# Cached keys turned by VectorE's block transpose, and raw buffers of 1,056 columns, in a hybrid streaming encoder step

## The chip, the core and the metric

The kernel runs on one core of a Trainium2 chip. A core has five engines that run side by side, each in the order of its own instruction list: TensorE (PE in the profile, with its weight loads as PEld), VectorE (DVE), ScalarE (ACT), GpSimd (POOL) and SyncE (SP). SyncE issues every transfer of this kernel; the transfers run on 16 DMA engines, in the order in which they were issued. The metric is the device time of one execution in microseconds; smaller is better.

## The reference

One inference step of a one-layer encoder, width 1024, on a prompt of 1024 rows and on eight running streams with 16 new rows each. All values are float32.

```python
# mixers, on the same normalised input
sq, sk, sv, fq, fk, fv, fg, z, xbc, dt = split_last(u @ w_in, IN_SIZES)
sb_o  = stick_breaking(sq, concat(cache_sb_k, sk), concat(cache_sb_v, sv))   # 4 heads of 64
fox_o = forgetting_softmax(fq, concat(cache_fox_k, fk), ..., log_gates)       # 4 heads of 64
ssd_o = rmsnorm(ssd_scan(...) * silu(z))                                       # 8 heads of 64
h = h + concat(sb_o, fox_o, ssd_o) @ w_out
# cross-attention, 4 heads of 256, 256 memory rows
q = rmsnorm(h) @ wq_x
h = h + softmax(q @ mem_k.T / 16) @ mem_v @ wo_x
# feed-forward
h = h + (silu(u @ w_gate) * (u @ w_up)) @ w_down
```

The prompt has no past. Each of the eight streams has 1024 cached rows of keys and values for both attention mixers, and its own 256 rows of memory keys and values for the cross-attention (`cache_mem_k`, `cache_mem_v`). All caches are stored with rows along the first axis, while a product of queries with keys needs the keys with the head's columns along the 128 partitions. The turning of these cached keys is what the change is about.

## The kernel before

The rows of the prompt and the streams, 1152 together, form nine blocks of 128 (the ninth holds the streams) or three chunks of 384. Dense products run in split precision: each float32 operand becomes a high part in a reduced format and a low part that holds the rest, and a product takes three matmuls (`mm3`, lines 328 to 330: high by high, high by low, low by high). A weight is loaded to a raw buffer, cast by ScalarE to the high part (L292) and subtracted by GpSimd for the low part (L132, in pieces of 256 columns). `w_unit` does this for one unit of weights.

The ring of buffers that all this goes through has four raw buffers of 528 columns (tag `wr`) and three each of 1,056 columns for the high and low parts (`wh`, `wl`). The decode also puts its turned keys (`kf`) and cached values (`vr`) into `wh` and `wl`.

The program is in one Python order with generators woven into each other, and a planner orders each engine's list by priorities and a simulated time line. Four stages touch the change:

- The first decode (stick-breaking, module 0) and the second (FoX, module 1), with prompt attention units around them. Each decode has four units of two streams; each unit calls `load_k` four times, for two halves of the cache and two streams, 32 calls in all. A call loads 512 rows of 256 columns with two transfers (L882), turns them with eight transposes on TensorE into PSUM (L888), and copies them out with two ScalarE copies (L890). Four products of 32 by 512 then run in four column groups of TensorE at once (L873).
- Dense projections fill the first decode; the SSD scan fills the second. It reloads its inputs by transfers from scratch in HBM (`act<-acsc`, `act<-xbcsc`, `act<-zsc`).
- The cross-attention goes head by head. `x_query` projects the queries of one head as two halves of 128 columns, with one weight unit of eight k-tiles by 128 columns for each half, while the attention of the head before is woven in (`both`, from `x_prompt` and `x_sample`).
- `x_sample` treats the eight streams of one head in two passes of four streams. In each pass it loads memory keys of two streams at a time (`mem_rows`, L1558), turns them by eight TensorE transposes (L1578), copies them by ScalarE and VectorE into `kf` (L1580), and multiplies (L1564). After the softmax it does the same with the memory values, which need no turning.

Elsewhere the raw buffers serve the weights of `w_out`, `wq_x` and `wo_x`, and one squares pass writes into one as scratch (L1804).

Of the kernel before, what the change touches and what calls it, by code (L numbers as in the profile page):

```python
# [62 lines left out]
def tile_hybrid_step(ctx: ExitStack, tc: tile.TileContext, a: dict):  # L63
# [239 lines left out]
    def raw_t():  # L303

        return ring.tile([P, 528], F32, tag="wr", name="wr", bufs=4)

    def w_unit(srcs, k0, nk, raw=None, pair=None, eng=POOL):

        n = sum(s[2] for s in srcs)
        raws = [raw_t(), raw_t()] if raw is None else [raw]  # L310
# [10 lines left out]
        for i, r in enumerate(raws):  # L321
            sl = slice(i * nk_ * n, (i + 1) * nk_ * n)
            split_into(hi[:, sl], lo[:, sl], r[:, :nk_ * n], eng)
# [516 lines left out]
    def decode_units(m):  # L840
# [15 lines left out]
        def rows(p):  # L856
# [19 lines left out]
            def load_k(hf, b2):  # L876
                rvs = []
                for q in range(2):
                    rvs.append(raw_t()[:, :512].rearrange("p (k c) -> p k c", c=256))
                    k0 = hf * 512 + q * 256  # L880

                    SP.dma_start(out=rvs[q], in_=ck[2 * p + b2, k0:k0 + 256, :].rearrange("(p k) c -> p k c", k=2))  # L882
                kf = ring.tile([P, 1056], F32, tag=("wh", "wl")[b2], name="kf")
                for q in range(2):
                    tp = pT()
                    for nb in range(2):
                        for k in range(2):
                            PE.transpose(tp[:, (2 * nb + k) * P:(2 * nb + k + 1) * P], rvs[q][:, k, nb * P:(nb + 1) * P],  # L888
                                         ident)
                    ACT.copy(kf[:, :1024].rearrange("c (n q p k) -> c n q p k", n=2, q=2, k=2)[:, :, q],  # L890
                             tp.rearrange("c (n k p) -> c n p k", n=2, k=2))
# [546 lines left out]
    def x_query(hd, out):  # L1438
# [5 lines left out]
        def job(db):  # L1444
# [7 lines left out]
            return ((2 * hd + db) * P, consume)  # L1452
        for db in range(2):
            yield from dense_T(wq, uc, [job(db)])

    def x_softmax(ps, n, pr):
# [3 lines left out]
        for i in range(n):  # L1460
            ACT.activation(pr[:, i * 256:(i + 1) * 256], ps[:, i, :], AF.Exp, bias=mx[:, n + i:n + i + 1],
# [7 lines left out]
    def x_mem(hd):  # L1469
# [78 lines left out]
    def x_sample(hd, q):  # L1548
        qs = q[2]
        for db in range(2):  # L1550
            POOL.tensor_copy(*put_streams(db, qs[:, db, :]))

        def mem_rows(src, b0):
# [3 lines left out]
            for b in range(2):  # L1557
                SP.dma_start(out=rv[:, b], in_=src[(b0 + 2 * b) * 256:(b0 + 2 * b + 1) * 256, hd * 256:(hd + 1) * 256]  # L1558
# [517 lines left out]
```

## Time and profile before

| what | value |
|---|---|
| median of three runs | 1884.5 us (1882.29 to 1886.88) |
| profiled execution | 1882.33 us |
| its span | 1880.6 us |
| granted TensorE clock | 0.994 |
| TensorE busy | 1826.0 us, 97% |
| VectorE, ScalarE, GpSimd busy | 886.7, 802.5, 618.4 us |
| DMA | 296.64 MB in 291,036 packets, 49.9% of 16 engines |

Busy times of different engines overlap, so they don't add up to the span. A row of a group names the line, the engine, the operation, the buffer written and read, the shape, the count, then the busy time in us and the mean of one in ns, then the idle time just before and what ended it. Matmuls are pipelined: the mean of one holds its latency, and the distance from one start to the next is what it costs in a dense row of them. A DMA packet is one contiguous run of bytes.

### The profile page before, as it was taken

How to read it: one execution, taken by the hardware profiler on the slowest of the kernel's cores; microseconds unless marked ns; L12 is line 12 of the kernel's file. 1: busy time of each engine (PE TensorE's matmuls, PEld its weight loads, DVE VectorE, ACT ScalarE, POOL GpSimd, SP SyncE). 2: the span in 40 equal slices, each digit the busy share in tenths (PEclk: the TensorE clock that was granted, in tenths of full speed). 3: DMA queues.
4: the chain of work that ended last, by engine and by line, in shares of the span. 5: the costliest groups of instructions: out<-in, count | busy, mean ns of one | idle time of the engine just before them, and what ended most of it. 6: DMA issues, size and time to landing. Idle time of an engine off the chain costs nothing.

```text
span 1880.6 us, 32355 instructions
## 1 busy us (share of the span) xinstructions
PE 1826.0 (97%) x12136; PEld 1632.1 (87%) x12136; DVE 886.7 (47%) x1798; ACT 802.5 (43%) x1719; POOL 618.4 (33%) x921
## 2 busy tenths in 40 slices
PE   7999998999999999999999989999999999999998
PEld 5899877888967768899988889999999999888886
DVE  3412323475657862444443596333333334455554
ACT  6533543545456861344432464333333333344443
POOL 7622424445116663101112107445444542000000
PEclk9999999999999999999999999999999999999999
DMA  9465654437588882245585124333222223657572
GB/s 333 153 188 152 210 144 130 144 109 205 175 262 266 281 288 91 108 134 177 173 284 191 68 73 119 90 85 76 71 71 71 71 71 93 217 184 246 171 247 86
DMA packets 291036, 296.64 MB, mean 158 GB/s; under 512 B 80060, under 2 KB 242852, under 8 KB 290880
## 3 DMA queue, kind: packets, MB, share of 16 engines
q1 hardware_dynamic: 290880, 294.57, 49.9%
q8 instruction: 96, 1.57, 0.3%
q14 instruction: 60, 0.49, 0.1%
HBM read 225.12 MB, written 69.91 MB: 157 GB/s over the span
## 4 chain that ended last, share of the span: by engine, by line
PE 83%; DMA 5%; DVE 4%; POOL 3%; ACT 2%; issue 2%; SPq 0%; DVEq 0%; POOLq 0%; ACTq 0%
PE psd L1869 11%; PE psd L328 10%; PE psd L329 10%; PE psd L330 10%; PE pst L1869 8%; PE pss L1869 4%; PE pss L328 4%; PE pss L329 4%; PE pss L330 4%; PE pso L1869 2%; PE pst L328 2%; PE pst L329 2%; PE pst L330 2%; PE pso L593 1%; DMA act<-acsc 1%
## 5 line engine op out<-in xcount | busy, mean ns | idle before, releaser
L132 POOL TENSOR_TENSOR wl<-wr,wh 128x256 fp32r<-128x256 f32 (+2 forms) x184 | 142.3, 807 | 229.5 <-ACT wh L292 208.6
L328 PE MATMUL psd<-act,wh 128*128 128x384 f32 x528 | 182.3, 346 | 0.0
L330 PE MATMUL psd<-act,wl 128*128 128x384 f32 x528 | 181.2, 343 | 0.6 <-POOL wl L132 0.6
L329 PE MATMUL psd<-act,wh 128*128 128x384 f32 x528 | 181.7, 344 | 0.0
L1869 PE MATMUL pst<-bT,tr 128*128 128x256 f32 (+1 forms) x1068 | 155.0, 293 | 0.0
L1869 PEld LDWEIGHTS pst<-bT,tr 128*128 128x128 f32 x1068 | 144.9, 188 | 0.1
L330 PE MATMUL psd<-wh,act 128*128 128x512 f32 (+3 forms) x424 | 136.7, 323 | 0.0
L329 PE MATMUL psd<-wl,act 128*128 128x256 f32 (+3 forms) x414 | 134.0, 324 | 1.9 <-POOL wl L132 1.9
L328 PE MATMUL psd<-wh,act 128*128 128x256 f32 (+3 forms) x414 | 132.9, 325 | 0.7 <-DMA act<-osc 0.5
L1869 PE MATMUL psd<-bT,tr 128*128 128x320 f32 (+1 forms) x912 | 132.8, 295 | 0.6 <-POOL tr L132 0.6
L1869 PEld LDWEIGHTS psd<-bT,tr 128*128 128x128 f32 x912 | 124.7, 188 | 1.0 <-POOL tr L132 0.9
L132 POOL TENSOR_TENSOR tr<-u,tr 128x256 fp32r<-128x256 f32 x110 | 82.8, 781 | 101.7 <-ACT tr L1705 83.8
L253 POOL TENSOR_SCALAR sm<-sm 128x1 f32<-128x1 f32 (+2 forms) x27 | 9.1, 337 | 298.4 <-ACT y L1980 209.0
L1844 DVE TENSOR_TENSOR tr<-tr,pst 128x256 f32<-128x256 f32 (+1 forms) x86 | 38.6, 449 | 139.9 <-ACT tr L1841 106.6
L330 PEld LDWEIGHTS psd<-act,wl 128*128 128x128 f32 x528 | 99.2, 188 | 3.2 <-issue 1.9
L132 POOL TENSOR_TENSOR ws<-ws 128x256 f32<-128x256 f32 (+2 forms) x100 | 69.2, 719 | 98.7 <-DVE ws L522 90.4
L328 PEld LDWEIGHTS psd<-act,wh 128*128 128x128 f32 x528 | 99.4, 188 | 2.5 <-issue 1.8
L329 PEld LDWEIGHTS psd<-act,wh 128*128 128x128 f32 x528 | 99.3, 188 | 1.9 <-issue 1.5
L132 POOL TENSOR_TENSOR tr<-raw,tr 128x256 fp32r<-128x256 f32 x94 | 69.2, 764 | 83.8 <-ACT tr L1705 75.7
L1705 ACT CAST tr<-u 128x512 fp32r<-128x512 f32 x130 | 76.8, 620 | 28.6 <-PE pst L1869 5.6
L292 ACT CAST wh<-wr 128x512 fp32r<-128x512 f32 (+2 forms) x90 | 52.4, 621 | 82.9 <-PE psd L330 32.1
L329 PEld LDWEIGHTS psd<-wl,act 128*128 128x128 f32 x414 | 78.9, 191 | 10.0 <-POOL wl L132 3.6
(645 smaller groups left out, 4674.4 us busy)
## 6 DMA issues: line engine op xcount, KB each, us to landing
u<-w_down SPq DMA_DIRECT2D x40, 512.0 KB
raw<-w_down SPq DMA_DIRECT2D x26, 512.0 KB
st<-qksc SPq DMA_DIRECT2D x48, 256.0 KB
wr<-w_in SPq DMA_DIRECT2D x44, 256.0 KB
tr<-hidsc SPq DMA_DIRECT2D x55, 192.0 KB
hidsc<-tr SPq DMA_DIRECT2D x34, 288.0 KB
qksc<-sg SPq DMA_DIRECT2D x48, 192.0 KB
wr<-cache_sb_k SPq DMA_DIRECT2D x32, 256.0 KB
```

Of the source, the lines that this page charges most:

```text
L132: POOL.tensor_tensor(out=out[:, a0:a1], in0=in0[:, a0:a1], in1=in1[:, a0:a1], op=op)
L253: POOL.tensor_scalar(v, ss, inv, EPS, ALU.mult, ALU.add)
L292: ACT.copy(hi, raw)
L328: PE.matmul(out, ah, bh, start=start, stop=False)
L329: PE.matmul(out, ah, bl, start=False, stop=False)
L330: PE.matmul(out, al, bh, start=False, stop=stop)
L593: return PE.matmul(po[r:r + 64, q_], vt[:, 2 * (k0 + i) + j, :], pfs[i][:, sl], start=start and k0 == 0 and (j == 0 or qp > 0), stop=k0 + ...
L1705: ACT.copy(hi, src)
L1844: DVE.tensor_tensor(out=at(out, g), in0=at(x, g), in1=ps[g][:, :GW[g]], op=op)
L1869: PE.matmul(dst[g][:, :GW[g]], x[:, ka], y[:, k, :], start=start and k == 0 and m == 0, stop=stop and k == 3 and m == 2, skip_group_check= ...
```

## The change

Three things change together.

The 32 calls of `load_k` load the same 512 rows with four transfers instead of two, one for each group of 32 partitions, so that partition and column already hold the right 32 by 32 blocks; each run in HBM is 32 floats long. One VectorE block transpose (`DVE.transpose`, which turns every 32 by 32 block of a 128 by 1024 tile by itself) writes the turned keys. The TensorE transposes and ScalarE copies go.

`x_sample` does the same for the memory keys, with four transfers in runs of 64 floats per two streams and one block transpose in its own buffer, and its products read every second column of it. The order of columns that follows (even columns of the head in the first half, odd ones in the second) is met by the query weights: `x_query` now loads both halves of a head as two units of four k-tiles by 256 columns, and `split_parted` sorts even and odd columns while it splits. The streams' order within a head and the memory rows' order in the softmax are permuted to match, in instructions that were there before. `kf` no longer takes `wh` and `wl` in `x_sample`.

The raw buffers become two of 1,056 columns, and `w_unit` uses the halves of one.

```diff
     def raw_t():
-        return ring.tile([P, 528], F32, tag="wr", name="wr", bufs=4)
+        return ring.tile([P, 1056], F32, tag="wr", name="wr", bufs=2)
+    def split_parted(hi, lo, raw):
+        h, l = (t.rearrange("p (k x m) -> p k x m", x=2, m=P) for t in (hi, lo))
+        r = raw.rearrange("p (k m x) -> p k x m", x=2, m=P)
+        ACT.copy(h, r)
+        for k in range(h.shape[1]):
+            POOL.tensor_tensor(out=l[:, k], in0=r[:, k], in1=f32(h[:, k]), op=ALU.subtract)
...
-        raws = [raw_t(), raw_t()] if raw is None else [raw]
+        if raw is None:
+            raw = raw_t()
+            raws = [raw[:, :528], raw[:, 528:]]
+        else:
+            raws = [raw]
...
             def load_k(hf, b2):
-                rvs = []
-                for q in range(2):
-                    rvs.append(raw_t()[:, :512].rearrange("p (k c) -> p k c", c=256))
-                    k0 = hf * 512 + q * 256
-                    SP.dma_start(out=rvs[q], in_=ck[2 * p + b2, k0:k0 + 256, :].rearrange("(p k) c -> p k c", k=2))
+                raw = raw_t()[:, :1024]
+                src = ck[2 * p + b2, hf * 512:(hf + 1) * 512, :].rearrange("(i t) (n g j) -> g i (t n) j", t=16, n=2, g=4)
+                for g in range(4):
+                    SP.dma_start(out=raw[32 * g:32 * g + 32].rearrange("i (b j) -> i b j", j=32), in_=src[g])
                 kf = ring.tile([P, 1056], F32, tag=("wh", "wl")[b2], name="kf")
-                for q in range(2):
-                    tp = pT()
-                    for nb in range(2):
-                        for k in range(2):
-                            PE.transpose(tp[:, (2 * nb + k) * P:(2 * nb + k + 1) * P], rvs[q][:, k, nb * P:(nb + 1) * P],
-                                         ident)
-                    ACT.copy(kf[:, :1024].rearrange("c (n q p k) -> c n q p k", n=2, q=2, k=2)[:, :, q],
-                             tp.rearrange("c (n k p) -> c n p k", n=2, k=2))
+                DVE.transpose(kf[:, :1024].rearrange("c (n i t) -> c t n i", n=2, t=16), raw)
                 return kf
...
+        units = [w_unit([(wq, 256 * hd, 256)], k0, 4, parted=True) for k0 in (0, 4)]
         for db in range(2):
-            yield from dense_T(wq, uc, [job(db)])
+            _, consume = job(db)
+            for c in range(NCH):
+                ps = pd()
+                uh, ul = uc[c]
+                for k in range(KT):
+                    wh, wl = (t[:, k % 4, db * P:(db + 1) * P] for t in units[k // 4])
+                    mm3(ps[:, :CW], wh, wl, uh[:, k, :], ul[:, k, :], k == 0, k == KT - 1)
+                consume(c, ps[:, :CW])
+                flush()
+                yield
...
             for i0 in (0, 2):
-                rv = mem_rows(cmk, 2 * i0 + e)
-                kf = ring.tile([P, 1056], F32, tag=("wh", "wl")[i0 // 2], name="kf")
-                for b in range(2):
-                    tp = pT()
-                    for db in range(2):
-                        for mb in range(2):
-                            PE.transpose(tp[:, db * 256 + mb * P:db * 256 + (mb + 1) * P],
-                                         rv[:, b, mb, db * P:(db + 1) * P], ident)
-                    (DVE.tensor_copy if b else ACT.copy)(kf[:, b * 512:(b + 1) * 512], tp)
-                kfs.append(kf)
+                raw = ws_t()[:, :1024]
+                k0 = (4 * e + i0) * 256
+                for g in range(4):
+                    SP.dma_start(out=raw[32 * g:32 * g + 32].rearrange("i (t c) -> i t c", c=64),
+                                 in_=cmk[k0:k0 + 512, hd * 256 + 64 * g:hd * 256 + 64 * g + 64]
+                                 .rearrange("(i t) c -> i t c", t=16))
+                blocks = raw.rearrange("p (t j x) -> p t x j", x=2, j=32)
+                DVE.transpose(blocks, blocks)
+                kfs.append(raw.rearrange("p (t i x) -> p x t i", x=2, i=32))
                 if i0:
-                    products(ps, e, lambda i, x: kfs[i // 2][:, i % 2 * 512 + x * 256:i % 2 * 512 + (x + 1) * 256])
+                    products(ps, e, lambda i, x: kfs[i // 2][:, x, :, i % 2 * 16:i % 2 * 16 + 16])
...
-                PE.transpose(tp[:, db * 256 + mb * P:db * 256 + (mb + 1) * P], mkn[:, mb, db * P:(db + 1) * P], ident)
+                PE.transpose(tp[:, db * 256 + mb * P:db * 256 + (mb + 1) * P], mkn[:, mb, db::2], ident)
```

More of the change, by code (lines that the diff above doesn't have):

```diff
@@ L303, in raw_t, with w_unit @@
     def raw_t():
[L305 to L310 removed]
+        return ring.tile([P, 1056], F32, tag="wr", name="wr", bufs=2)
[5 more added lines that the diff above has]
+            POOL.tensor_tensor(out=l[:, k], in0=r[:, k], in1=f32(h[:, k]), op=ALU.subtract)
+    def w_unit(srcs, k0, nk, raw=None, pair=None, eng=POOL, parted=False):
+        n = sum(s[2] for s in srcs)
+        if raw is None:
[3 more added lines that the diff above has]
+            raws = [raw]
         nk_ = nk // len(raws)
@@ L322, in w_unit @@
             sl = slice(i * nk_ * n, (i + 1) * nk_ * n)
-            split_into(hi[:, sl], lo[:, sl], r[:, :nk_ * n], eng)
+            if parted:
+                split_parted(hi[:, sl], lo[:, sl], r[:, :nk_ * n])
+            else:
+                split_into(hi[:, sl], lo[:, sl], r[:, :nk_ * n], eng)
         return (hi[:, :nk * n].rearrange("p (k n) -> p k n", n=n),
@@ L1460, in x_softmax @@
         for i in range(n):
-            ACT.activation(pr[:, i * 256:(i + 1) * 256], ps[:, i, :], AF.Exp, bias=mx[:, n + i:n + i + 1],
+            to, of = pr[:, i * 256:(i + 1) * 256], ps[:, i, :]
+            if blocks:
+                to, of = to.rearrange("q (i t) -> q t i", t=blocks), of.rearrange("q (t i) -> q t i", t=blocks)
+            ACT.activation(to, of, AF.Exp, bias=mx[:, n + i:n + i + 1],
                            accum_out=su[:, i:i + 1])
@@ L1550, in x_sample @@
         for db in range(2):
-            POOL.tensor_copy(*put_streams(db, qs[:, db, :]))
+            dst, _ = put_streams(db, qs[:, db, :])
+            POOL.tensor_copy(dst, qs[:, db, :].rearrange("p (e i t) -> p i e t", e=2, t=DEC_S))
         def mem_rows(src, b0):
@@ L1557, in mem_rows @@
             for b in range(2):
-                SP.dma_start(out=rv[:, b], in_=src[(b0 + 2 * b) * 256:(b0 + 2 * b + 1) * 256, hd * 256:(hd + 1) * 256]
+                SP.dma_start(out=rv[:, b], in_=src[(b0 + b) * 256:(b0 + b + 1) * 256, hd * 256:(hd + 1) * 256]
                              .rearrange("(m p) c -> p m c", p=P))
@@ L1562, in products, with out @@
         def products(ps, e, moving):
-            together([lambda i=i, x=x, b=2 * i + e: PE.matmul(
-                ps[32 * i:32 * i + 32, :256], zq[:, x, 32 * b:32 * b + 32], moving(i, x),
+            def out(i, m):
+                o = ps[32 * i:32 * i + 32, :256]
+                return o if len(m.shape) == 2 else o.rearrange("p (t i) -> p t i", i=DEC_S)
+            together([lambda i=i, x=x, b=2 * i + e, m=moving(i, x): PE.matmul(
+                out(i, m), zq[:, x, 32 * b:32 * b + 32], m,
                 start=e == 0 and x == 1, stop=e == 1 and x == 0) for x in (1, 0) for i in (3, 0, 1, 2)])
@@ L1601, in x_sample @@
         for db in range(2):
-            PE.transpose(tp[:, db * P:(db + 1) * P], on[:, db * P:(db + 1) * P], ident)
+            PE.transpose(tp[:, db * P:(db + 1) * P].rearrange("p (e i t) -> p i e t", e=2, t=DEC_S),
+                         on[:, db * P:(db + 1) * P], ident)
         x_out(hd, (tp[:, 0:P], tp[:, P:2 * P]), SEQ, P)
```

8 lines of the change are left out of this document (4 added, 4 removed).

## The prediction

> **What bounds the kernel now.** I read the page first, its busy shares and its chain of waits, and then the windows of the stages.
>
> ```profile
> span 1880.6 us, 32355 instructions
> ...
> PE 1826.0 (97%) x12136; PEld 1632.1 (87%) x12136; DVE 886.7 (47%) x1798; ACT 802.5 (43%) x1719; POOL 618.4 (33%) x921
> ...
> PE 83%; DMA 5%; DVE 4%; POOL 3%; ACT 2%; issue 2%; SPq 0%; DVEq 0%; POOLq 0%; ACTq 0%
> ```
>
> TensorE is busy 97% of the span and carries 83% of the chain that ended last. Work taken from it is worth its full price where nothing else is close behind. Where that holds is read from the stages: 188 to 435 us holds the stick-breaking decode, 515 to 705 the forgetting (FoX) decode beside the SSD scan, 800 to 990 most of the cross-attention. Each row has the stretch, its length, the busy time (and instructions) of PE, PEld, DVE, ACT and POOL, the granted clock, the DMA share and GB/s.
>
> ```profile
> 188.00:435.00 247.00, 233.21 (x1778) 202.58 (x1776) 110.22 (x191) 116.19 (x269) 100.01 (x156) 0.99 0.51 149
> 435.00:515.00 80.00, 79.37 (x591) 73.80 (x587) 49.06 (x102) 37.72 (x87) 33.49 (x53) 1.00 0.65 190
> 515.00:705.00 190.00, 177.33 (x1471) 134.84 (x1471) 132.83 (x381) 123.69 (x275) 97.67 (x156) 0.99 0.84 275
> 705.00:800.00 95.00, 95.00 (x437) 77.67 (x436) 36.55 (x64) 28.07 (x51) 26.04 (x39) 1.00 0.30 103
> 800.00:990.00 190.00, 189.48 (x1403) 176.57 (x1402) 89.17 (x210) 75.14 (x203) 22.15 (x37) 1.00 0.58 193
> ```
>
> The cross-attention is TensorE's alone: 189.5 of 190 us busy, DMA at 58%. The first decode is nearly so (94%, DMA 51%). The FoX stage is different: TensorE has 12.7 us idle, its weight loads cover only 135 of 190 us, VectorE is at 70%, and the 16 DMA engines are at 84%. Its chain of waits says the same:
>
> ```profile
> by line: DMA act<-acsc 13.4%; issue 5.2%; PE pst L578 4.7%; PE pso L593 4.1%; DMA wr<-cache_fox_k 4.0%; DMA s_ssm<-act 3.0%; DVE act L1079 3.0%; DMA act<-mixsc 2.9%; POOL act L1030 2.8%; DVE act L1085 2.7%; DMA act<-zsc 2.6%; ACT act L1077
> ...
> 514.49 7.56 DMA wr<-cache_fox_k
> ```
>
> There the transfers named add up to 26% of the chain, and one key load takes 7.56 us from issue to use. So this stage must be asked about DMA, the other two about TensorE.
>
> **What is removed.** 256 transposes in `load_k` (L888; 32 calls, 8 each) and 128 in `x_sample` (L1578; 16 units, 8 each), with the copies out of PSUM behind them.
>
> ```profile
> L888 PE MATMUL pst<-ident,wr 128*128 128x128 f32 x256 | 38.2, 278 | 3.9 <-DMA wr<-cache_sb_k 2.7 <-ACT kf L890 0.8 <-DMA wr<-cache_fox_k 0.3
> L890 ACT COPY kf<-pst 128x512 f32<-128x512 f32 x64 | 36.2, 593 | 17.4 <-PE pst L888 13.6 <-PE pss L873 3.2
> L1578 PE MATMUL pst<-ident,ws 128*128 128x128 f32 x128 | 20.7, 273 | 0.0
> L1580 DVE COPY kf<-pst 128x512 f32<-128x512 f32 x16 | 10.9, 687 | 2.5 <-PE pst L1578 1.7 <-PE psd L329 0.5
> L1580 ACT COPY kf<-pst 128x512 f32<-128x512 f32 x16 | 9.4, 589 | 6.9 <-PE pst L1578 6.0 <-PE psd L329 0.7
> L271 DVE TENSOR_SCALAR ws<-ws,sm 128x1024 f32<-128x1024 f32 x9 | 9.0, 1049 | 0.1
> L522 DVE TENSOR_TENSOR_SCAN ws<-ws 128x1024 f32<-128x1024 f32 x4 | 9.5, 2376 | 4.5 <-ACT ws L519 4.5
> L1564 PE MATMUL pss<-kf,ws 128*32 128x256 f32 x128 | 8.6, 385 | 0.0
> ```
>
> Busy time would make it 38.2 + 20.7 = 58.9 us. That is too much, since the busy time of a transpose includes its latency, which the next matmul overlaps. The timeline has the step between starts:
>
> ```profile
> 868.55 0.33 PE L328 MATMUL psd<-act,wh 128*128 128x384 f32 x1
> 868.72 0.34 PE L329 MATMUL psd<-act,wh 128*128 128x384 f32 x1
> 868.90 0.27 PE L1578 MATMUL pst<-ident,ws 128*128 128x128 f32 x1
> 868.92 0.42 PE L330 MATMUL psd<-act,wl 128*128 128x384 f32 x1
> 869.18 0.27 PE L1578 MATMUL pst<-ident,ws 128*128 128x128 f32 x1
> ...
> 341.95 1.03 PE L888 MATMUL pst<-ident,wr 128*128 128x128 f32 x8
> ```
>
> Two dense matmuls stand 0.17 us apart; transpose to transpose with one dense matmul between is 0.28, so a transpose costs 0.11. Eight in a row take 1.03, of which the last one's 0.27 is latency: 0.76/7 = 0.11. I take 0.11 us: 128 transposes are 14 us in each of the three stages, 42 us in all; 58.9 us is the upper end.
>
> ScalarE loses 36.2 + 9.4 us and VectorE 10.9 us of copies, which lie beside TensorE and count for nothing directly.
>
> **What is added on VectorE.** 48 block transposes of 128x1024, 32 for the decodes and 16 for the memory keys. No row shows one. The nearest of that size are a plain pass at 1.05 us (L271) and the scan at 2.38 us (L522); I take 1.1, since a transpose has no dependence from element to element as a scan has. In the FoX stage VectorE goes from 132.8 to 132.8 + 16 x 1.1 = 150 us of 190 (171 at 2.38); in the others it stays under 60%. It is hidden, and in its place the 0.59 us copy and the transposes before it fall away from each chain. Without that cover the price would be 16 x 1.1 = 18 us in the FoX stage. [...]
>
> **What is added on the DMA queue.** A key load was 2 transfers with runs of 2 KB; it becomes 4 with runs of 32 floats, 128 bytes. A memory-key unit goes from 2 transfers with 1 KB runs to 4 with 256-byte runs. The price per packet comes from windows that hold one kind of transfer: 384.3 to 384.8 us (a store of 128-byte runs, L959), 368.0 to 369.6 (a load of 256-byte runs, L510), 421.4 to 423.5 (a key load), 860.4 to 871.8 (memory rows). In each row: packets, MB, share of 16 engines.
>
> ```profile
> q1 hardware_dynamic: 274, 0.03, 43.5%
> ...
> q1 hardware_dynamic: 1040, 0.26, 72.2%
> ...
> q1 hardware_dynamic: 288, 0.52, 80.4%
> ...
> q1 hardware_dynamic: 3264, 3.15, 85.8%
> ```
>
> Share x window x 16 / packets gives 0.435 x 0.5 x 16 / 274 = 12.7 ns for 128 bytes, and likewise 17.8 ns for 256 bytes, 93.8 for 2 KB and 47.9 for 1 KB. These counts include 16 small packets per transfer. A key load was 2 x 144 packets x 93.8 / 16 = 1.7 us of the whole queue and becomes 4 x 1040 x 12.7 / 16 = 3.3 us. For 16 calls of one decode: 27 us become 53, +26. That a load of 128 bytes costs what the store does isn't shown; the 256-byte load bounds it at 17.8 ns without other traffic (74 us, +47), and half of that, 8.9, from below (+10). Memory keys: 16 x 544 x 47.9 / 16 = 26 us become 16 x 2112 x 17.8 / 16 = 38, +12.
>
> First decode: 126 us of DMA become 152 in 247; cross-attention: 110 become 122 in 190. Both are hidden. FoX stage: 0.84 x 190 = 160 become 186 in 190. TensorE alone would now allow 176, DMA needs 186 without a gap: I take the stage as unchanged, 0, between -14 and, at 17.8 ns, 207 - 190 = +17. Every call also issues two more transfers, 96 in all, on the one queue that carries everything. The VectorE transposes stand in order on their engine, so one that waits for its load holds up the SSD and softmax work behind it, where before it was TensorE that waited, little:
>
> ```profile
> L882 SPq DMA_DIRECT2D wr<-cache_fox_k x32: 328/383/2783, 468.5 to 653.4; - x32
> PE pst L888 <- DMA wr<-cache_sb_k: 2.7, 2, 1.5
> ```
>
> At 0.38 us (the median) the 96 issues are 37 us, spread over three stages of 627 us; what they delay is in the DMA sum.
>
> **What is moved.** Query weights come as two units of four k-tiles by 256 columns per head, both held until the second half of the head is done. Of three buffers one is free, so the next head's second unit is split only after the first unit's last use.
>
> ```profile
> L132 POOL TENSOR_TENSOR wl<-wr,wh 128x256 fp32r<-128x256 f32 x176 | 136.2, 806 | 229.5 <-ACT wh L292 208.6 <-PE pst L578 16.0 <-DMA wr<-wq_x 4.8
> L292 ACT CAST wh<-wr 128x512 fp32r<-128x512 f32 x82 | 47.6, 621 | 79.5 <-PE psd L330 32.1 <-DMA wr<-w_in 9.4 <-PE pss L1564 7.9
> ```
>
> The split takes one cast and four subtracts before all is ready, 0.62 + 4 x 0.81 = 3.9 us. Between release and need lie 24 dense matmuls (k 4 to 7 of the last group, k 0 to 3 of the next), 24 x 0.17 = 4.1 us, and attention work: hidden, 1 us at most. Without the cover it is 3 x 3.9 = 12 us. The raw buffers, two of 1,056 for four of 528, come free with the second half's split instead of the first's, two subtracts or 1.6 us later; prefetched loads hide that. The softmax and output permutations keep their instruction counts.
>
> **The sum.** First decode -14, and -1 for waits of TensorE on L888's loads and copies; FoX 0; cross-attention -14 + 1 = -13. Together -28. The profiled execution took 1882.3 us (1.7 around its span): 1854. The median of the runs, 1884.5, is 2 higher, so 1855 is what I expect of a median.
>
> **Rivals.** *B, the FoX stage gives its share too:* loads go out early (the first are issued at 468.5, with DMA at 65% there), and the copies and PSUM tiles no longer waited for shorten its chain: 14 more, 1841, down to about 1830 if the transposes are worth their busy time. Against it: 186 us of transfers in 190. *C, the wait moves to VectorE:* if each of the 16 FoX loads shows its extra 3.3 - 1.7 = 1.6 us on the path, the stage grows by 26: about 1881. For it: the 7.56 us load and the 26% of the chain in transfers; against: `load_k` has two raw buffers and runs ahead.
>
> *D, slower: 128-byte loads are dear.* The FoX stage without its key loads holds 160 - 27 = 133 us of DMA; its new loads are 66,560 packets, 4160 per engine. The gain of 28 is gone once 133 us + 4160 c = 218 us, c = 20.5 ns. At twice the store's price, 25.4 ns, the stage takes 239: +49 - 28 = +21, 1904 us by the profiled execution. For it: these rows are stores or loads in quiet windows, and in the stage the queue is contended. Against: the 256-byte load at 17.8 moves twice the bytes. [...]
>
> **Chances.** Forecast 0.5 (own range 1842 to 1868), B 0.2, C 0.15, D 0.15. The range 1832 to 1884 reaches over B and C and leaves out D and B's far end. A difference under 0.2%, 3.8 us, can't be told from none. Faster: forecast, B and a third of C, 0.75; same: half of C, 0.08; slower: D and the rest, 0.17.
>
> **What would show it.** Right: TensorE's busy time about 50 us lower, the cross-attention and first decode each 13 to 15 us shorter, 128-byte packets near 13 ns, the FoX stage at 98% DMA and as long as before. Wrong: transposes of 2 us or more on VectorE with TensorE idle before L873; L535 or the SSD lines waiting behind them; a FoX stage well over 200 us with DMA above 95% throughout; or TensorE idle before the query matmuls for POOL's splits.

## The result

The change makes the kernel slower: 1928.1 us median of four runs (1923.6 to 1933.7), against 1884.5 before (four runs, 1882.3 to 1886.9). The ratio is 1.023, with a 95% interval of 1.022 to 1.025. The prediction said 1855 us, with a range from 1832 to 1884. The profiled execution took 1923.6 us for 1882.3.

The page of the kernel after:

```profile
span 1921.8 us, 31580 instructions
...
PE 1818.4 (95%) x11752; PEld 1612.9 (84%) x11752; DVE 964.3 (50%) x1830; ACT 762.6 (40%) x1639; POOL 618.6 (32%) x921
...
DMA packets 435929, 296.59 MB, mean 154 GB/s; under 512 B 245436, under 2 KB 395940, under 8 KB 435776
...
q1 hardware_dynamic: 435776, 294.58, 53.9%
```

All 384 transposes are gone from TensorE's count (12,136 to 11,752), but its busy time fell by 7.6 us only, and the span grew by 41.2. So TensorE now waits 49 us more in all, and what work is left takes longer.

I cut the span at three points that can be found in every kernel: the last scan of the first decode (L522 before), the first sum of the output projection (L1322), which ends the FoX stage, and the first feed-forward product (L1869). The feed-forward part behind them takes 786.1 us before and 786.9 after. The columns are the stretch, its length, busy time (and instructions) of PE, PEld, DVE, ACT and POOL, the granted clock, the DMA share and GB/s. First the windows of before, then those of after:

```profile
188.00:455.60 267.60, 253.18 (x1890) 221.15 (x1889) 122.80 (x204) 125.97 (x291) 113.56 (x172) 0.99 0.53 155
455.60:701.60 246.00, 234.07 (x1933) 187.94 (x1932) 165.91 (x462) 149.57 (x334) 117.61 (x192) 0.99 0.78 251
701.60:1094.50 392.90, 391.63 (x2372) 342.19 (x2373) 183.47 (x386) 144.94 (x354) 67.95 (x103) 1.00 0.45 151
```

```profile
188.00:455.60 267.60, 246.72 (x1772) 214.99 (x1765) 152.82 (x219) 111.16 (x262) 118.00 (x175) 0.94 0.60 152
455.60:729.30 273.70, 237.81 (x1803) 184.65 (x1801) 200.77 (x477) 134.76 (x303) 116.15 (x192) 0.92 0.85 225
729.30:1134.90 405.60, 387.69 (x2245) 335.13 (x2245) 189.93 (x388) 136.22 (x338) 67.83 (x104) 0.97 0.50 147
```

Three things can be read from each row: the length, TensorE's idle time (length less busy) and its clock. The record of the granted clock knows two values, 1.0 and 0.5; the column is their mean, so half of the busy time spent at half clock is taken as lost work: in the trace of after, a 128x128 transpose starts 0.11 us behind the one before it at full clock, and 0.21 us at half clock. The first row of the table counts idle time from TensorE's first matmul on.

| stage | length | idle of TensorE | time at half clock |
|---|---|---|---|
| start to end of first decode | 455.6 to 455.6 | 20.2 to 27.5 | 6.8 to 30.7 |
| FoX | 246.0 to 273.7 | 11.9 to 35.9 | 3.4 to 44.4 |
| rest of output projection, cross-attention | 392.9 to 405.6 | 1.3 to 17.9 | 0 to 20.5 |

Take 14 us for the transposes out of each row, add the new idle time and half of the new time at half clock: FoX gives -14 + 24.0 + 20.5 = +30.5 against 27.7 measured, the cross-attention -14 + 16.6 + 10.3 = +12.9 against 12.7, the first decode -14 + 7.3 + 12.0 = +5 against 0. The books close to about 5 us, since part of the half-clock time is idle time and is counted twice here.

Without that part, TensorE is busy at half clock for 22.0, 41.0 and 15.8 us after, and for 6.4, 3.4 and 0 before. With half of this taken off, its busy time falls by 15.5, 14.9 and 11.9 us, 42 in all. This estimate of the work that went is what the prediction had priced. Beside it stand two losses that the prediction had put at nothing: waits of TensorE, and a clock that falls behind them.

### The profile page after: what moved, and what is told of

The parts are those of the page before. It is cut to its first block, busy times and chain, and to the rows that moved or that the text cites. A ratio compares the mean times of both kernels' runs of the same rounds, so it can differ in the third digit from the quotient of the medians.

```text
span 1921.8 us, 31580 instructions
## 1 busy us (share of the span) xinstructions
PE 1818.4 (95%) x11752; PEld 1612.9 (84%) x11752; DVE 964.3 (50%) x1830; ACT 762.6 (40%) x1639; POOL 618.6 (32%) x921
## 5 line engine op out<-in xcount | busy, mean ns | idle before, releaser
L132 POOL TENSOR_TENSOR wl<-wr,wh 128x256 fp32r<-128x256 f32 (+2 forms) x152 | 118.0, 809 | 260.3 <-ACT wh L292 251.0
L342 PE MATMUL psd<-act,wh 128*128 128x384 f32 x528 | 182.7, 346 | 1.0 <-DVE sg L470 1.0
L342 PE MATMUL psd<-wh,act 128*128 128x256 f32 (+3 forms) x414 | 136.7, 334 | 4.8 <-DMA act<-osc 2.8
L342 PEld LDWEIGHTS psd<-act,wh 128*128 128x128 f32 x528 | 99.7, 189 | 5.5 <-issue 1.9
L342 PEld LDWEIGHTS psd<-wh,act 128*128 128x128 f32 x414 | 81.8, 198 | 15.7 <-DMA act<-osc 3.7
L344 PEld LDWEIGHTS psd<-wh,act 128*128 128x128 f32 x424 | 83.4, 197 | 11.2 <-DMA act<-osc 4.1
```

The costliest lines, as they stand in the source:

```text
L132: POOL.tensor_tensor(out=out[:, a0:a1], in0=in0[:, a0:a1], in1=in1[:, a0:a1], op=op)
L342: PE.matmul(out, ah, bh, start=start, stop=False)
L344: PE.matmul(out, al, bh, start=False, stop=stop)
```

## What the new waits look like

These are the groups of after for the new transposes and for the memory products (the 256 of the last row are those with the keys and those with the values):

```profile
L896 DVE STREAM_TRANSPOSE kf<-wr 128x1024 f32<-128x1024 f32 x32 | 61.0, 1940 | 41.8 <-PE psd L343 10.5 <-DMA wr<-cache_sb_k 9.1 <-DMA wr<-cache_fox_k 8.6
...
L1602 DVE STREAM_TRANSPOSE ws<-ws 128x1024 f32<-128x1024 f32 x16 | 19.9, 1244 | 20.6 <-DMA ws<-cache_mem_k 20.4 <-DVE st L1454 0.2
...
L1587 PE MATMUL pss<-ws 128*32 128x256 f32 x256 | 16.4, 387 | 3.1 <-DMA act<-osc 3.1
```

A decode transpose takes 1.94 us and VectorE stands 41.8 us idle ahead of the 32 of them, some of it for loads. What stands behind such a wait is seen in the first decode. VectorE's timeline and a wait of TensorE in the same stretch of after:

```profile
239.43 1.90 DVE L896 STREAM_TRANSPOSE kf<-wr 128x1024 f32<-128x1024 f32 x1 [4.35 <-DMA wr<-cache_sb_k]
241.18 0.17 DVE L506 TENSOR_TENSOR lf<-psd,hb 128x4 f32<-128x4 f32 x2
```

```profile
PE psd L342 <- DVE lf L506: 1.9, 1, 1.9
```

VectorE waits 4.35 us for a key load. Behind it in VectorE's order stands a pass of 0.17 us that empties a PSUM tile (L506), and TensorE's next dense product (L342) waits 1.9 us for that tile. Before, this unit's transposes stood later in time (from 247.7 us on); two of them waited for their load, 1.5 and 1.1 us, and the pass (L492 there) had no transpose ahead of it. In after it is TensorE's only wait between 238.9 and 242.2 us; yet the record of the clock shows half clock for 3.4 us from 242.2 us on.

The largest such place follows. Windows of after, 14, 2, 24 and 12 us long, and then one form of transpose from groups within 276.5 to 299 us and within 312 to 388 us:

```profile
260.00:274.00 14.00, 13.68 (x106) 10.88 (x104) 4.53 (x8) 7.67 (x20) 5.63 (x7) 1.00 0.48 149
274.00:276.00 2.00, 0.00 (x0) 0.00 (x0) 2.00 (x3) 0.93 (x2) 2.00 (x2) 1.00 1.09 366
276.00:300.00 24.00, 15.33 (x65) 12.57 (x66) 18.26 (x42) 6.57 (x15) 15.04 (x28) 0.51 0.46 59
300.00:312.00 12.00, 10.23 (x135) 9.41 (x133) 0.51 (x3) 0.60 (x3) 0.00 (x0) 0.99 0.28 100
```

```profile
L929 PE MATMUL pst<-ident,ws 128*128 128x128 f32 x9 | 2.4, 427 | 3.2 <-POOL ws L132 3.2
...
L592 PE MATMUL pst<-ident,ws 128*128 128x128 f32 x54 | 9.0, 274 | 0.1
```

A stop of 3.2 us is followed by 24 us at half clock, and the same transpose takes 427 ns there and 274 at full clock. Over the 16 traces of this case, of the idle times of TensorE of 2.5 us and more that began at full clock (without the one behind its first matmul), 56 of 61 were followed by half clock within 7 us of their start; of those between 1 and 1.5 us, 36 of 104. In the traces of before and after alone it is 8 of 8 and 2 of 11, and there the stretches at half clock last 3.41, 6.83, 13.65 and 23.89 us, multiples of 3.41, but for one at the very end of each kernel (6.1 and 5.8 us). What makes the clock fall isn't shown, but the stop ahead can be shorter than such a stretch: in the 3.4 us ahead of the fall at 242.2 us, TensorE stood idle for 1.9 us only.

In the FoX stage the products of queries with keys, of the prompt (L574) and of the caches (L887), wait for VectorE's softmax passes (L549), the first of them 12 times (waits of TensorE, and of VectorE's transposes, 456 to 730 us):

```profile
PE pss L574 <- DVE sm L549: 13.7, 12, 2.5
...
PE pss L887 <- DVE sm L549: 3.4, 3, 2.3
```

```profile
DVE kf L896 <- DMA wr<-cache_fox_k: 8.6, 3, 4.2
```

Before, the longest wait of TensorE in that stage was 2.9 us, and of the two lines' matmuls (L560 and L873 there) only the second's waited for that pass, 0.4 us:

```profile
PE psd L1094 <- ACT sg L1169: 2.9, 1, 2.9
...
PE pss L873 <- DVE sm L535: 0.4, 1, 0.4
```

And the transfers fill the queue. The same stretch of time, 576 to 624 us (not the same work, since the stage is longer after), as its share of 16 engines (packets, MB, share), before and after:

```profile
q1 hardware_dynamic: 9266, 11.51, 74.6%
```

```profile
q1 hardware_dynamic: 25076, 12.14, 102.2%
```

## Experiments: the two parts, and the raw buffers

**The decodes alone.** The new `load_k` and raw buffers; the cross-attention as before.

```diff
-                    SP.dma_start(out=rvs[q], in_=ck[2 * p + b2, k0:k0 + 256, :].rearrange("(p k) c -> p k c", k=2))
...
+                for g in range(4):
+                    SP.dma_start(out=raw[32 * g:32 * g + 32].rearrange("i (b j) -> i b j", j=32), in_=src[g])
...
+                DVE.transpose(kf[:, :1024].rearrange("c (n i t) -> c t n i", n=2, t=16), raw)
```

> Only load_k and the raw buffers are changed; the cross-attention is that of the kernel before. By the stage marks of the two profiles (last stick-breaking scan 455.6 us in both, first w_out sum 701.6 against 729.3) the two decodes should carry +28 us of the +41: about 1912 us. If the loss sat in the cross-attention instead, this run would be near 1885.

Measured 1917.6 us, ratio 1.0168 (1.0153 to 1.0183): +32 us. First decode +7.1, FoX +28.6, cross-attention +1.4 in the profiles.

**The cross-attention alone**, with `load_k` and raw buffers as before.

```diff
+                blocks = raw.rearrange("p (t j x) -> p t x j", x=2, j=32)
+                DVE.transpose(blocks, blocks)
```

> Only the cross-attention is changed; load_k and the raw buffers are those before. From the first w_out sum to the first feed-forward matmul the profiles have 392.9 us before and 405.6 after: +13, about 1897 us. The loss should lie between the seventh query group and the feed-forward (the last head), and the heads before should be faster by some 18 us. If the decode's late DMA or the raw buffers had caused it, this run would be 13 to 18 us faster than before, about 1868.

Measured 1883.3 us, ratio 0.9984 (0.9968 to 0.9999): no difference that can be told. Its two halves can be told apart by windows, from the end of the FoX stage to the seventh query group of the cross-attention, before and in this run:

```profile
702.00:951.00 249.00, 248.66 (x1563) 222.69 (x1563) 110.20 (x236) 89.96 (x215) 41.93 (x65) 1.00 0.41 137
```

```profile
710.00:940.00 230.00, 229.33 (x1391) 205.32 (x1395) 107.87 (x214) 79.14 (x188) 44.95 (x69) 1.00 0.50 137
```

With TensorE full and hardly a wait, the way to that point is 19 us shorter. Some 14 of these are the transposes: over the whole stage TensorE's busy time, brought to full clock, falls from 391.7 to 378.1 us. The rest is work that now lies behind that point. From there to the feed-forward part it takes 162 us for 143.5. Part of this is that work (the x counts), and part is waiting: 7.3 us idle and 13.7 us at half clock, where before there were 0.5 and none. Two waits make most of it:

```profile
PE pss L1592 <- DVE ws L1607: 3.3, 1, 3.3
PE psd L338 <- DMA act<-osc: 2.6, 1, 2.6
```

**The last head by TensorE.** The run above, with the last head's memory keys loaded in 1 KB runs and turned by TensorE.

```diff
+                if hd == 3:
+                    rv = mem_rows(cmk, 4 * e + i0)
...
+                                PE.transpose(tp[:, db * 256 + mb * P:db * 256 + (mb + 1) * P], rv[:, b, mb, db::2], ident)
```

> e2_cross_only with the memory keys of the last of the four heads loaded in 1 KB runs and turned by TensorE as before. In e2 the marks say 19 us gained up to the seventh query group and 18 lost from there to the feed-forward. If the loss comes from the last head's 256-byte loads arriving in a full queue, this run keeps most of the 19 and is 1866 to 1874 us. If the loss comes from the earlier heads being faster (the stores and loads between attention and output product have less time), it stays at 1880 or more.

Measured 1888.1 us, ratio 1.0002 (0.9984 to 1.002). The profile has no half clock left in the stage, but 9.0 us of idle time stay, now for softmax passes and copies. The time is no shorter than with all heads on VectorE, so taking the last head's own small loads away doesn't cure the loss.

```profile
PE pss L338 <- ACT pt L1484: 2.9, 2, 1.7
PE pso L339 <- DVE pt L1551: 2.0, 1, 2.0
```

**Earlier reloads in the cross-attention.** The cross-attention alone, with the reloads for the last product started one step of the prompt attention sooner.

```diff
-X0, X1, XL = 2, 2, 2
+X0, X1, XL = 2, 1, 2
```

> The cross-attention part alone (1883), with the reloads of the attention output for the last product issued one step of the last head earlier. If the 8 us of idle time and 13.7 us at half clock of that stage come from these loads being late, most of it goes and the time is 1870 to 1876. If they come from the shorter cover (the transposes were TensorE's work while VectorE, ScalarE and the memory loads finished), the time stays at 1880 to 1886.

Measured 1885.7 us, ratio 0.9993 (0.9978 to 1.0007), with 10.3 us idle and 10.2 us at half clock in the stage. TensorE still waits 2.1 us for such a reload, for 2.6 in the run above, so earlier reloads bring little, and late ones aren't shown to be the cause. That the transposes were themselves the cover of the last head's waits fits this run and the one before; it isn't shown directly.

**The old raw buffers.** The whole change with four buffers of 528 columns; a key load is then eight transfers and two transposes of 128x512.

```diff
-        return ring.tile([P, 1056], F32, tag="wr", name="wr", bufs=2)
+        return ring.tile([P, 528], F32, tag="wr", name="wr", bufs=4)
...
+                for q in range(2):
+                    DVE.transpose(kf[:, :1024].rearrange("c (n i t) -> c t n i", n=2, t=16)[:, 8 * q:8 * q + 8], raws[q])
```

> The whole change, but with four raw buffers of 528 as before; load_k takes two and turns each with a transpose of 128x512, with eight transfers for four. e1 and e2 add up to 1885.7 + 32 - 2 = 1915, the change takes 1928: 13 more together than apart. Theory ring (the raw buffers released as one delay the weights of the output product in the last head): 1910 to 1918. Theory schedule (it is the order that the planner finds): no better than 1924.

Measured 1914.7 us, ratio 1.015 (1.0132 to 1.0168): 13 us better than the change (15 by the ratios). The two profiles are 9.7 us apart, 9.5 of them behind the FoX stage (cross-attention 396.1 us for 405.6; FoX 274.2 for 273.7). The parts alone add up to +32 - 3 = +29, the change measured +44. This run accounts for the difference by the raw buffers, or by the shorter transfers and transposes that come with them. How they hinder the new cross-attention isn't shown.

## Experiments: what makes the decodes slower

These runs go from before to the decodes alone in steps. The cross-attention is as before in all of them.

**No turning at all.** The 256 transposes are left out; ScalarE's copies take the rows unturned.

```diff
-                            PE.transpose(tp[:, (2 * nb + k) * P:(2 * nb + k + 1) * P], rvs[q][:, k, nb * P:(nb + 1) * P],
-                                         ident)
-                    ACT.copy(kf[:, :1024].rearrange("c (n q p k) -> c n q p k", n=2, q=2, k=2)[:, :, q],
-                             tp.rearrange("c (n k p) -> c n p k", n=2, k=2))
+                    ACT.copy(kf[:, :1024].rearrange("c (n q p k) -> c n q k p", n=2, q=2, k=2)[:, :, q],
+                             rvs[q].rearrange("c k (n p) -> c n k p", n=2))
```

> The kernel before with the 256 transposes of the decodes' cached keys left out: the two ScalarE copies of a load take the unturned rows from the raw buffers, so the scores of cached keys are wrong, and loads, buffers, copies and products stay as they were. If a transpose on TensorE is worth 0.11 us with nothing behind it, as the prediction has it, both decode stages lose about 14 us and the time is near 1857. If the transposes were cover, so that TensorE then waits for softmax passes and loads, and drops to half clock behind such waits, the stages lose under 5 us together and the time is 1878 to 1886, with more idle time of TensorE than the 20.2 and 11.9 us of before.

Measured 1882.6 us, ratio 0.9981 (0.9969 to 0.9993). With nothing turned, and ScalarE's copies kept, the decodes win 3.6 us (1.3 to 5.8 by the interval), where the price of the transposes is 28. Windows of the three stages in this run, and its longest wait in the FoX stage:

```profile
188.00:447.70 259.70, 243.25 (x1777) 213.16 (x1776) 128.63 (x207) 124.18 (x287) 117.33 (x175) 0.96 0.53 155
447.70:699.30 251.60, 226.03 (x1805) 176.78 (x1803) 166.04 (x464) 151.62 (x335) 117.90 (x192) 0.96 0.78 245
```

```profile
PE pss L560 <- DVE sm L535: 5.9, 5, 3.8
```

The first decode gains 8 us and the FoX stage loses 5.6. A loss of that size in one profile can't be told from none: in five other runs that leave the FoX decode as it was, the stage takes 245.7 to 253.3 us. What can be told is that it gains nothing. TensorE's work there, brought to full clock, falls by 15 us, its idle time goes from 11.9 to 25.6 us (11.4 to 17.6 in the five runs), and its time at half clock from 3.4 to 20.5 (0 to 20.5). TensorE's removed work turns into waits, the longest of them for a softmax pass.

**No turning, two raw buffers of 1,056.** The same, with the change's buffers.

```diff
-        return ring.tile([P, 528], F32, tag="wr", name="wr", bufs=4)
+        return ring.tile([P, 1056], F32, tag="wr", name="wr", bufs=2)
```

> The cached keys unturned (scores wrong) as in the first run without turning, 2 KB runs, ScalarE's two copies, but raw buffers of two by 1,056 columns. Against it stands the kernel with VectorE's transposes of the same loads in the same buffers, 1900 us. If VectorE's transposes, in order before its softmax passes, are the 18 us between the two, the time is 1881 to 1888. If the raw buffers are, it is 1896 to 1902.

Measured 1893.8 us, ratio 1.0028 (1.0011 to 1.0044). The expectation had the two readings far apart; the time falls between them. The buffers cost 0.47%, 9 us. (The differences between these runs are of their ratios; by the intervals, each step is uncertain by 4 to 6 us.) The FoX row shows where: 10.8 us longer, more than the 7.6 by which the five runs above differ, at a clock of 0.90, with 0.75 of DMA for 0.78.

```profile
444.70:707.10 262.40, 238.37 (x1805) 185.15 (x1803) 166.66 (x463) 151.93 (x335) 118.69 (x192) 0.90 0.75 235
```

**VectorE's transposes of 2 KB loads.** As the run before this, with the change's `DVE.transpose` in place of ScalarE's copies. The code is shown against the change, here and in the next three runs; in the decodes only the loads differ from it here.

```diff
-                for g in range(4):
-                    SP.dma_start(out=raw[32 * g:32 * g + 32].rearrange("i (b j) -> i b j", j=32), in_=src[g])
+                for q in range(2):
+                    k0 = hf * 512 + q * 256
+                    SP.dma_start(out=raw[:, q * 512:(q + 1) * 512].rearrange("p (k c) -> p k c", c=256),
+                                 in_=ck[2 * p + b2, k0:k0 + 256, :].rearrange("(p k) c -> p k c", k=2))
```

> load_k loads with two transfers in runs of 2 KB as before, and VectorE transposes 128x1024 as in the change; each 32 by 32 block is turned but the blocks are not where the product needs them, so the scores over the caches are of wrong keys. Theory VectorE: slow like e1, 1905 or more, with TensorE waiting on the FoX reductions. Theory DMA: no slower than before, 1870 to 1885.

Measured 1900.3 us, ratio 1.0074 (1.0051 to 1.0098), between the two readings of its expectation, so another 0.46%, 9 us, for VectorE's turning by itself, with transfers of the same size as before. In the profiles the first decode grows from 444.7 to 457.3 us and the FoX stage from 262.4 to 266.7; that is more than 9, since the profiled execution (1906.9 us) was the longest of its five. From here to the decodes alone it is 0.94%, 18 us, for the runs of 128 bytes.

**Small runs with TensorE's transposes.** The loads of the change, and buffers of the change, with eight transposes and two copies as before; the keys then stand in another order.

```diff
-                DVE.transpose(kf[:, :1024].rearrange("c (n i t) -> c t n i", n=2, t=16), raw)
+                for q in range(2):
+                    tp = pT()
+                    for k in range(4):
+                        PE.transpose(tp[:, k * P:(k + 1) * P], raw[:, q * 512 + k * P:q * 512 + (k + 1) * P], ident)
...
```

> load_k loads with four transfers in runs of 32 floats, but TensorE transposes and ScalarE copies stay as before; the keys come out in another order, so the attention over the caches is of permuted keys. Theory DMA (the small runs clog the queue): slow like e1, 1905 or more. Theory VectorE (the 1.94 us transposes in VectorE's order hold up TensorE): 1885 to 1895.

Measured 1932.9 us, ratio 1.0254 (1.0226 to 1.0282): worse than with VectorE's transposes. Waits of TensorE, 188 to 760 us:

```profile
PE pst L899 <- DMA wr<-cache_sb_k: 10.5, 6, 2.5
PE pst L899 <- DMA wr<-cache_fox_k: 6.5, 2, 5.4
```

Whichever engine turns the keys stands in its order and waits for the slower load. Small runs are a loss of their own, since the raw buffers explain 9 of these 48 us. This kernel is 16 us slower than the decodes alone; how much of that is TensorE's waiting and how much the 256 transposes, isn't told apart.

**Transfers over 128 partitions.** The decodes alone, with the same number of packets of the same size, but each of the four transfers spread over all partitions; the keys stand elsewhere.

```diff
-                    SP.dma_start(out=raw[32 * g:32 * g + 32].rearrange("i (b j) -> i b j", j=32), in_=src[g])
+                    SP.dma_start(out=raw[:, 256 * g:256 * g + 256].rearrange("p (b j) -> p b j", j=32),
+                                 in_=src[g // 2][:, g % 2 * 8:g % 2 * 8 + 8])
```

> e1_decode_only with one thing changed: each of the four key transfers goes to all 128 partitions and not to 32, with the same number of packets of 128 bytes; the keys come out in another order, so the scores over the caches are of wrong keys. In e1 and in the change 4096 packets took about 4 us (some 1050 packets per us). Theory spread (32 partitions at a time slow the transfer down): over 1200 packets per us, and 5 to 15 us faster than e1's 1917. Theory packets (their number costs, wherever they land): 1050 packets per us again, and 1910 to 1925 us.

Measured 1906.7 us, ratio 1.0113 (1.0087 to 1.014): 0.55%, 10 us, of the 18 aren't the size of the runs but come with transfers that fill 32 partitions only. No run here tells whether the partitions are the reason or something else, such as the order of the runs in HBM, which changes too.

**A contiguous write.** The decodes alone, with the transpose writing in order and the products reading in steps of 64 columns, 256 bytes.

```diff
-                DVE.transpose(kf[:, :1024].rearrange("c (n i t) -> c t n i", n=2, t=16), raw)
+                DVE.transpose(kf[:, :1024], raw)
...
+                    quads(ps, lambda b2, nb: kf[b2][:, :1024].rearrange("c (t n i) -> c n i t", n=2, t=16)[:, nb])
```

> e1_decode_only with the block transpose writing its columns in place order (no steps of 64 bytes), and the key products reading in steps instead. The cross-attention's transpose without such steps took 1.24 us against 1.94: 32 x 0.7 = 22 us of VectorE go. Theory VectorE: 8 to 20 us faster than e1, 1898 to 1910, if the products (L887, 0.6 us for four at once) don't double. Theory DMA: 1915 to 1920, VectorE only waits longer for the loads.

Measured 1923.3 us, ratio 1.0195 (1.017 to 1.0221).

```profile
L897 DVE STREAM_TRANSPOSE kf<-wr 128x1024 f32<-128x1024 f32 x32 | 39.1, 1235 | 51.3 <-PE pss L887 13.1 <-PE psd L343 12.0 <-DMA wr<-cache_sb_k 11.5
...
L887 PE MATMUL pss<-kf,st 128*32 128x512 f32 x64 | 19.2, 1290 | 0.1
```

The transposes fall to 1.24 us, but each product takes 1290 ns for 605 before. The time is above both ranges of the expectation, whose condition (products that don't double) wasn't met. The run mixes the two, so what shorter transposes alone would bring stays open.

## Experiments: where the first decode could gain

**The second unit by TensorE.** The whole change, with four of the 32 loads as before.

```diff
+                if m == 0 and p == 1:
...
+                        SP.dma_start(out=rq, in_=ck[2 * p + b2, k0:k0 + 256, :].rearrange("(p k) c -> p k c", k=2))
```

> The whole change, with the keys of the second unit of the first decode (four of 32 calls) loaded in 2 KB runs and turned by TensorE as before. In the change this unit is the one that grows (first values of unit 1 to unit 2: 80 us for 69), with TensorE waiting for VectorE and 24 us at half clock from 276 us on. If VectorE's transposes there cause these, the half-clock stretch is gone, the first decode ends 8 to 12 us earlier and the time is near 1918. If the wait merely moves to another unit or to the loads, the stage ends within 3 us of 455.6 and the time stays near 1928.

Measured 1908.4 us, ratio 1.0108 (1.0093 to 1.0123): four loads are worth 20 us, twice what was expected. The profiles show 14.6 of them: the first decode ends 10 us earlier, at 445.6, and the FoX stage takes 270.3 us for 273.7. VectorE's timeline shows a reason. L420 is a step in the chain that makes the forget gates, for whose end TensorE waits (L672, which ends at 287.1 us in the change); L536 are the long scans of stick-breaking. First after, then this run:

```profile
270.26 2.81 DVE L536 TENSOR_TENSOR_SCAN ws<-ws 128x1152 f32<-128x1152 f32 x1
...
273.68 0.38 DVE L420 RECIPROCAL sg<-sg 128x36 f32<-128x36 f32 x1
273.97 1.96 DVE L536 TENSOR_TENSOR_SCAN ws<-ws 128x896 f32<-128x896 f32 x1
...
278.13 2.54 DVE L536 TENSOR_TENSOR_SCAN ws<-ws 128x1024 f32<-128x1024 f32 x1
```

```profile
263.02 0.38 DVE L420 RECIPROCAL sg<-sg 128x36 f32<-128x36 f32 x1
...
277.83 2.72 DVE L536 TENSOR_TENSOR_SCAN ws<-ws 128x1152 f32<-128x1152 f32 x1 [6.62 <-ACT ws L533]
```

In the change the gate chain comes 11 us later than in this run and falls among the scans; from L420 to L672 it takes 13.4 us for 4.3. The 24 us at half clock begin at 276.3 us, ahead of its end, in the stop of 3.2 us shown above. TensorE's wait for the chain lies inside them, until 287.2 us:

```profile
PE psd L696 <- DVE lf L672: 5.6, 1, 5.6
```

With the second unit on TensorE the chain comes before those scans, and the first decode has 13.7 us at half clock for 30.7.

**Two units and the cross-attention.** Raw buffers as before; VectorE for the first and third unit of the first decode and for the memory keys, with the earlier reloads.

```diff
+                    if m == 0 and p in (0, 2):
...
+                        DVE.transpose(kf[:, :1024].rearrange("c (n i t) -> c t n i", n=2, t=16)[:, 8 * q:8 * q + 8], raw)
```

> A candidate for a better kernel: raw buffers as before (four of 528), memory keys by VectorE, the cached keys by VectorE only in the first and third unit of the first decode, all others by TensorE, and the earlier reloads of the run beside it. In the change the first unit ends 4 us earlier than before and the third takes 10 us less. If these gains are the units' own, the time is 10 to 14 us below that of the run beside it, 1860 to 1870. If each unit's gain is given back by the next (the stage's softmax passes and loads set its length), the time is within 4 us of the run beside it.

Measured 1889.8 us, ratio 1.0013 (0.9993 to 1.0032). At the third unit's values the profile is 11 us ahead of before (361.6 for 372.9), and the fourth unit gives nearly all of it back: the stage ends at 454.1.

**Three units.** The same without the new cross-attention and the earlier reloads, and with the fourth unit on VectorE too.

```diff
+                    if m == 0 and p != 1:
```

> The kernel before with the cached keys of three units of the first decode (first, third, fourth) by 128-byte loads and VectorE, the second unit, the FoX stage and the cross-attention by TensorE, and raw buffers as before. With all four in these places and the second by TensorE, the whole change ended this stage at 445.6 us for 455.6. If that gain is the stage's own, nothing behind it changes and the time is 1874 to 1879. If the next stage takes it back (its loads and scans are not ready earlier), or the halved raw buffers slow the loads, the time is within 4 us of before.

Measured 1879.6 us, ratio 0.9955 (0.9938 to 0.9972): 8 us (0.45%) faster than before, and the only complete kernel of this study that is clearly so. The windows of its three stages:

```profile
188.00:448.70 260.70, 245.51 (x1798) 217.27 (x1795) 134.97 (x220) 115.01 (x270) 111.74 (x174) 0.97 0.58 156
448.70:695.50 246.80, 233.33 (x1933) 186.35 (x1931) 166.48 (x462) 149.64 (x334) 116.85 (x192) 1.00 0.79 251
695.50:1090.70 395.20, 393.73 (x2372) 343.30 (x2373) 183.80 (x388) 144.63 (x355) 67.38 (x103) 1.00 0.45 150
```

The first decode is 6.9 us shorter than before, and the next stage, unchanged, is as long as it was; the third, also unchanged, is 2.3 us longer in this profile.

## Why the prediction was wrong, by its steps

**The step that failed** is a reading that the prediction used twice: that busy shares show what an engine can give up for gain or take on for nothing.

First, it says that work taken from TensorE "is worth its full price where nothing else is close behind", and finds such places by busy shares of 94% and more. It counted on 15 us in the first decode. With all 256 transposes of the decodes gone and no new work, 3.6 us of the priced 28 appeared in the two stages together. The work did go, as priced; but in the first decode and the FoX stage TensorE's order is tied to softmax chains and loads, and waits and half clock took its place.

Second, it put the new work at nothing where an engine or the queue had room by its sum: VectorE's transposes "hidden", the small runs 0 on the path, the raw buffers covered because "prefetched loads hide that". In the decodes these cost 9, 18 and 9 us.

Of the 72 us between the forecast of -28 and the 44 measured, the first use of the reading makes 11 (-4 for -15), the second 36, and the cross-attention the other 25. There the step held up to the last head: some 14 us of the 19 gained to that point are the transposes, as priced for the whole stage. The last head gave most of it back (3 us were left in the cross-attention alone), and the change's raw buffers, or what comes with them, cost the other 15. (The sum's last step has a slip: 1854 and 2 make 1856, not 1855.)

**The clock** was missing. The prediction took each wait at its own length. In the change TensorE's granted clock fell from 0.994 to 0.972, and the half-clock time of the three stages rose from 10.2 to 95.6 us. Half of the busy part of the increase is 34 us of lost work, beside 48 us of new idle time.

**VectorE's transposes** were taken at 1.1 us and hidden. The decodes' took 1.94, between the ends of 1.05 and 2.38, the memory keys' 1.24. The price was within bounds; "hidden" was wrong, since a share of 70% says nothing on order. With equal loads and buffers, turning on VectorE costs 9 us more than leaving the keys unturned with ScalarE's copies. This is in part rival C's mechanism, a wait that moves to VectorE; but C's 26 us were the longer loads, which this step doesn't have.

**The small runs** were put at +26 us of DMA in the FoX stage, with 0 for the path and +17 at the upper end. Stage length times DMA share gives 0.78 x 246 = 192 us before and 0.85 x 273.7 = 233 after, +41. The price of a packet held: in the change those of 128 bytes took 13 ns at the median, for 12.7. What failed is that they cost the path nothing. They cost the whole kernel 18 us; the profiles show 5.4 of it in the first decode and 7.8 in the FoX stage. About half of it went away with transfers that fill 128 partitions, a difference that the prediction hadn't priced. Rival D was right that the runs cost time, and its 1904 us was the nearest of the four, but it can't stand for the result: without small runs the decodes are already slower than before.

**The raw buffers** were costed at nothing ("prefetched loads hide that"). They cost 9 us without any turning, and 13 to 15 in the whole change. The two aren't the same cost: with the old buffers the whole change is better only behind the FoX stage, and its decodes stay as slow.

**The query weights** held: no wait for a split shows in the cross-attention of after. The memory products read in steps of 8 bytes after the change, for which the sum had no cost, and they took 387 ns for 385 (the 387 holds the products with the values too).

**The signs** named for a wrong forecast came nearly as stated: transposes near 2 us, lines behind them waiting, a FoX stage well over 200 us with DMA above 95% in its middle, though not throughout. Of the signs for a right one, only the packets near 13 ns came.

The terms, as differences of ratios times 1886 us: transposes removed -4, raw buffers +9, VectorE's turning +9, small runs +18, and the cross-attention with its share of the buffers +12. They add up to the 44 measured, because they are steps from one kernel to the next. They aren't free of the schedule: each edit also lets the planner order other work anew, and how much of a step of 9 us is that order, no run here tells.

## What to carry to other kernels

Before an engine's work is priced as gain, leave it out altogether and time that: here it showed that 28 us of transposes were worth 4. A busy share below full says nothing on what stands next in an engine's order. A wait on a load should stand on the engine with the fewest urgent lines behind it, since an engine that works in order passes the wait on, as VectorE's 4.35 us for a key load became 1.9 us of TensorE in the change; that is advice from these waits, which no run tests alone. For TensorE, count a wait of 2.5 us or more with the half clock, which followed such idle times in 56 of 61 cases here.

## What the hardware showed that was not expected

- Idle times of TensorE of 2.5 us and more were followed by half clock in 56 of 61 cases. The longest stretch in the change was 24 us, with a transpose at 427 ns for 274.
- A block transpose of 128x1024 float32 takes 1.24 us when it writes in order or in steps of 8 bytes, and 1.94 us in steps of 64 bytes. A product whose moving operand is read in steps of 256 bytes takes 1290 ns for 605.
- Packets of 128 bytes, as many as before, cost the kernel 10 us less when each transfer fills 128 partitions instead of 32; the order of the runs in HBM changed with it.
